# Dividing attention outputs by the softmax sums, which pass through DRAM, instead of scaling the probabilities

## The chip, the core and the metric

The kernel runs on one core of a Trainium2 chip. The metric is device time in microseconds (us), the median of the runs of one program. Five engines work side by side, each through its own instructions in a fixed order: TensorE (PE, with its weight loads as PEld), VectorE (DVE), ScalarE (ACT), GpSimd (POOL) and SyncE (SP, which here only issues DMAs). An engine that comes to an instruction whose inputs are not ready waits, and all that stands behind it waits too.

## The reference

One layer of a decoder on 16 meta tokens and 512 real ones, 1024 features wide, in float32: a gated feed-forward block, a token mixer with two attention branches, a second feed-forward block. The change is in the two attentions.

```python
def one_block(args):                                   # forgetting attention ("fox"), 8 heads of 64
    s = jnp.einsum('bqhd,bkhd->bhqk', qi, k) * scale
    s = s + cqi[..., :, None] - c_k[:, :, None, :]
    s = jnp.where(mask[None, None], s, NEG)
    pr = jax.nn.softmax(s, axis=-1)
    return jnp.einsum('bhqk,bkhd->bqhd', pr.astype(v.dtype), v)
...
# sliding window ("swa"), 8 query heads on 2 key heads, with a sink per head
mx = jnp.maximum(jnp.max(s, axis=-1, keepdims=True), sink)
pr = jnp.exp(s - mx)
pr = pr / (jnp.sum(pr, axis=-1, keepdims=True) + jnp.exp(sink - mx))
out = (jnp.einsum('bngrqk,bnkgd->bnqgrd', pr[..., :2 * BLOCK], vb)
       + jnp.einsum('bngrqm,bmgd->bnqgrd', pr[..., 2 * BLOCK:], vm))
...
y = jax.nn.sigmoid(ga) * (o_fox @ w_branch_fox) + jax.nn.sigmoid(gb) * (o_swa @ w_branch_swa)
return y @ w_out
```

## The kernel before

[...] A factor is split in a high half (a cast, `hi`, by ACT, L133) and a low half (what the cast left, `lo`, by DVE, L140), and PE adds high by high, high by low and low by high (`prod`, L301, L302, L304). Weights come from DRAM by SP in pieces of up to 512 KB into `raw`, which has three buffers (L252, L206); ACT makes `wh` from it, DVE `wl`, and a buffer comes free, and the next load goes out, when `wl` is made.

The program runs through the first feed-forward block, the projections and attentions of the mixer, the gates and output products, and the second feed-forward block. The attentions are sixteen units of work, first eight of `fox_pair` (two heads and two blocks of 128 queries; `p` counts the pairs of heads, `ip` the pairs of blocks, 1 before 0), then eight of `swa_unit` (four heads `g` and one block `i`). Each unit has these steps:

- `scores`: PE multiplies queries and keys (L1292 in fox, L301 to L304 in swa); DVE adds bias and mask, scales, writes the score tile `t` and its negated row maximum `nmx` (L1310, L1460); then `normalise`, which the change takes apart. There ACT makes the exponentials in place and their row sums `l` (L1209, a sum per query, and the queries lie on the partitions), DVE inverts the sums (L1210) and scales each tile by its own (L1212).
- `turn`: PE transposes `t` by a product with the identity (L1337 and L1350 in fox, L1473 in swa), ACT and DVE split the result in `pH` and `pL`. Now the keys lie on the partitions.
- `values`: PE multiplies `pH` and `pL` with the values `v` (L1359, L1364, L1365; L1488, L1490). The two halves of the partitions of the result are added into the output `oA` by ACT (L1105, a copy to `hsq`) and DVE (L1106). In `oA` the features lie on the partitions and the queries along the row, so a query's sum is no longer a scalar of a partition.

Between these steps stand fills, pieces of projections and gate products that have nothing to do with the unit (`weave`, L57): the turn and the values of a unit come after the scores of the next one, with fills between. The projections end in `head_norm`: ACT squares (L1057), DVE sums and adds (L1058, L1059), POOL takes the power (L351), DVE scales into `qn` (L1073). Within this frame the instructions of all engines are laid out when the program is built, by when each is thought to be ready, so that a changed step can move its neighbours. Loads and stores of ACT and SP stand in the same fixed order as the rest of their engine's work.

A tile `zA` takes the gates later; its rows 6 and 7 hold biases for fox, and its rows 0 to 3 are unused until the gates are made. After the attentions ACT reads `xg` from DRAM (L1700) into room that the attention's tiles leave.

Of the kernel before, what the change touches and what calls it, by code (L numbers as in the profile page):

```python
# [11 lines left out]
F32 = mybir.dt.float32  # L12
# [7 lines left out]
P = 128  # L20
# [5 lines left out]
NB = S // P  # L26
# [56 lines left out]
def kernel(  # L83
# [32 lines left out]
    def nm(s):  # L116
        nid[0] += 1
        return f"{s}_{nid[0]}"
# [339 lines left out]
    class Units:  # L458
# [5 lines left out]
        def new(self, tag, bufs, w=1):  # L464
            return self.pool.tile([P, w * self.th], F32, tag=tag, name=nm(tag), bufs=bufs)
# [633 lines left out]
    def both_halves(o, rows_, ps):  # L1099

        other = slice(64 - rows_.start, 128 - rows_.start)
        tmp = new("hsq", [P, 256], F32, 3)[rows_, :256]
        if len(ps.shape) > 2:
            tmp = tmp.rearrange("p (a q) -> p a q", q=P)
        A.copy(tmp, ps[other])  # L1105
        V.tensor_tensor(out=o, in0=ps[rows_], in1=tmp, op=ALU.add)  # L1106
# [95 lines left out]
        G.tensor_copy(lt[:, S:], ct[:, :M])  # L1202
        A.dma_start(cbd[0::2], lt[0:8:2])

    def normalise(parts):

        l = new("l", [P, 4], F32, 2)[:, : len(parts)]
        for j, (t, nmx) in enumerate(parts):
            shared["exp"] = A.activation(t, t, AF.Exp, bias=nmx, scale=-1.0, accum_out=l[:, j : j + 1])  # L1209
        V.reciprocal(l, l)  # L1210
        for j, (t, _) in enumerate(parts):
            V.tensor_scalar(t, t, l[:, j : j + 1], None, op0=ALU.mult)  # L1212


    cbs = {}
# [33 lines left out]
    def fox_pair(box, p, ip, before):  # L1249
# [7 lines left out]
        def scores():  # L1257
            before()
            q, k = box["q"], box["k"]
            main, last = cbs[p]  # L1260
            a, b = [main[:, :MAIN], last[:, : 2 * P]], [main[:, MAIN : 2 * MAIN], last[:, 2 * P :]]
            if ip:
                blocks = [
                    [[(P + M, MAIN, 0, 0, a[0])], [(0, MAIN, 0, 0, b[0])]],
                    [
                        [(LAST, LAST, 0, 2 * P, a[0][:, P:]), (M, 2 * P, 0, 0, a[1])],
                        [(0, LAST, 0, 0, b[0]), (LAST, 2 * P, 0, LAST, b[1])],
                    ],
                ]
            else:  # L1270
                w = 2 * P - P - M
                blocks = [
                    [[(3 * P + M - w, 2 * P, w, 0, a[1])], [(0, 2 * P, 0, 0, b[1])]],
                    [[(LAST, LAST, 0, 0, a[0][:, P:])], [(0, LAST, 0, 0, b[0])]],
                ]
            if ip:
                room = [new("t", [P, 1092], F32) for _ in range(2)]
            else:
                t = new("t0", [P, 2 * (keys[0] + keys[1] + M)], F32, 1)
                room = [t[:, : 2 * keys[0] + M], t[:, 2 * keys[0] + M :]]  # L1280
            for t, nk in zip(room, keys):
                G.memset(t[:, nk : nk + M], 0.0)
                ts_.append(t)
            pss = {}
            for b, block in enumerate(blocks):
                i = 2 * ip + b
                for pi in range(len(block[0])):
                    two = pss[b, pi] = psum(), psum()
                    for qx, kx in ((0, 0), (0, 1), (1, 0)):
                        for hb, ps, spans in zip(half, two, block):  # L1290
                            c0, w = spans[pi][:2]
                            PE.matmul(  # L1292
                                ps[:, :w],
                                q[qx][hb, hp, P * i : P * i + P],
                                k[kx][hb, hp, c0 : c0 + w],
                                start=qx + kx == 0,
                                stop=qx == 1,
                            )
            parts = []
            for hh in range(2):  # L1300
                for b, block in enumerate(blocks):
                    nk = keys[b]
                    t = ts_[b][:, (nk + M) * hh : (nk + M) * hh + nk]
                    nmx = new("nmx", [P, 2], F32, 8)
                    init = 3.0e38
                    for pi, (_, w, skip, to, cb) in enumerate(block[hh]):
                        n = min(w - skip, nk)
                        if not ip and b == 0:
                            n = nk
                        V.tensor_tensor_reduce(  # L1310
                            out=t[:, to : to + n],
                            in0=pss[b, pi][hh][:, skip : skip + n],
                            in1=cb[:, :n],
                            scale=-0.125,
                            scalar=init,
                            op0=ALU.add,
                            op1=ALU.min,
                            accum_out=nmx[:, pi : pi + 1],
                        )
                        init = nmx[:, pi : pi + 1]  # L1320
                    parts.append((t, init))
            for hh in range(2):
                normalise(parts[2 * hh : 2 * hh + 2])

        def column(hh, j, b):

# [28 lines left out]
        def values(hh):  # L1355
            v = box["v"]
            pv = psum()
            h0 = P * (2 * hp + hh)
            PE.matmul(pv[:, : 2 * P], v[:, 0, h0 : h0 + P], pts[0][:, : 2 * P], start=True, stop=False)  # L1359
            for j in range(1, nt):  # L1360
                pH, pL, c0 = pts[j]
                st = v[:, j, h0 : h0 + P]
                a = P if j == nt - 1 else 0
                PE.matmul(pv[:, a:256], st, pH[:, c0 + a : c0 + 256], start=False, stop=False)  # L1364
                PE.matmul(pv[:, a:256], st, pL[:, c0 + a : c0 + 256], start=False, stop=j == nt - 1)  # L1365
            both_halves(oA[half[hh], 0, p, 2 * P * ip : 2 * P * (ip + 1)], half[hh], pv[:, :256])

        return [scores] + [lambda f=f, hh=hh: f(hh) for hh in range(2) for f in (turn, values)]

# [61 lines left out]
    def swa_unit(box, qbox, g, i, before):  # L1431
# [8 lines left out]
        def scores():  # L1440
# [3 lines left out]
            for hp in range(2):  # L1444
                t2 = room[:, 546 * hp : 546 * hp + 546]
                for hh in (2 * hp, 2 * hp + 1):
# [16 lines left out]
                        )  # L1463
                        init = nmx[:, pi : pi + 1]
                    ts_.append((t, init))
            normalise(ts_)
            ts_[:] = [t for t, _ in ts_]

        def turn():
            for tt, c0 in tiles:  # L1470
# [12 lines left out]
        def values():  # L1483
            v = box["v"]
            pv = psum()
            for j, ((tt, c0), (pH, pL)) in enumerate(zip(tiles, pts)):
                st = v[:, tt, P * g : P * g + P]
                PE.matmul(pv, st, pH, start=j == 0, stop=False)  # L1488
                if tt:
                    PE.matmul(pv, st, pL, start=False, stop=j == len(tiles) - 1)  # L1490
            pvv = pv.rearrange("p (a b q) -> p a b q", b=2, q=P)
            for par in range(2):
                hb = slice(64 * par, 64 * par + 64)
                both_halves(o[hb, :, P * i : P * i + P], hb, pvv[:, :, par])

        return [scores, turn, values]

# [520 lines left out]
```

## Time and profile before

| what | us |
|---|---|
| median of three runs | 1078.03 (1077.87 to 1078.66) |
| the profiled execution | 1079.11 |
| its span, first to last instruction | 1076.5 |
| first scores of fox (L1292) | from 412.5 |
| first scores of swa (L1460) | from 520.1 |
| last of swa's scores begins (L1460) | 586.2 |
| load of xg (L1700) | 597.0 |

The granted clock of PE is 1.00 all through. In a row of a timeline the first number is the start and the second the duration, both in us; then come engine, line, operation, what is written and read, the shape, and in brackets the idle time of the engine just before and what ended it. In a row of groups the numbers behind the bar are the busy time in us and the mean of one in ns. "q" behind an engine marks what its sequencer issues. Line numbers are those of the kernel before, except where the changed program is shown.

### The profile page before, as it was taken

What the parts mean: (1) busy time and instruction counts of PE and PEld (TensorE: products, weight loads), DVE (VectorE), ACT (ScalarE), POOL (GpSimd) and SP (SyncE); (2) the same over time, 40 slices, a digit from 0 to 9 for tenths busy, and PEclk for the clock granted to TensorE, in tenths of its full rate; (3) what the DMA queues carried; (4) which work ended last, traced back from release to release, by engine and by line L of the source; (5) the groups of instructions that cost most, each with busy time, mean ns of one, the idle gap of its engine ahead of it and who ended that gap; (6) DMA issues with size and microseconds to landing.
All of it is one profiled execution on the core that took longest, in us unless ns stands there. A gap on an engine that the chain in (4) does not pass through costs nothing.

```text
span 1076.5 us, 22257 instructions
## 1 busy us (share of the span) xinstructions
PE 1063.5 (99%) x8515; PEld 1030.4 (96%) x8515; DVE 891.7 (83%) x1725; ACT 654.0 (61%) x1235; POOL 211.1 (20%) x280
## 2 busy tenths in 40 slices
PE   8999999999999999999999999999999999999998
PEld 8999999999999999999877799999999999999998
DVE  7988878888889678789897799688989788887895
ACT  7667456656666455556657776455665466645664
POOL 3011111121124442332200110001122211221120
PEclk9999999999999999999999999999999999999999
DMA  8787777688776314212211874557688877877763
GB/s 283 198 219 161 188 191 197 152 218 218 176 180 176 121 60 129 73 58 80 81 59 50 237 185 118 195 186 199 172 201 179 192 191 182 176 187 195 159 125 102
DMA packets 112299, 173.57 MB, mean 161 GB/s; under 512 B 10865, under 2 KB 59249, under 8 KB 111809
## 3 DMA queue, kind: packets, MB, share of 16 engines
q1 hardware_dynamic: 74032, 122.03, 35.7%
q0 software_dynamic: 28768, 37.83, 22.7%
q10 hardware_dynamic: 9392, 12.29, 3.6%
q8 instruction: 66, 1.08, 0.4%
q14 instruction: 41, 0.33, 0.1%
HBM read 167.89 MB, written 6.32 MB: 162 GB/s over the span
## 4 chain that ended last, share of the span: by engine, by line
PE 45%; DVE 5%; ACT 3%; DMA 2%; issue 1%; POOL 0%; ACTq 0%; DVEq 0%; POOLq 0%
PE ps L301 8%; PE ps L304 8%; PE ps L302 8%; PE pt L301 6%; PE pt L302 6%; PE pt L304 6%; DMA raw<-in_wout_dram 1%; DVE wl L140 1%; ACT wh L133 1%; DMA xg<-h1d 1%; ACT t L1209 1%; DVE pL L140 1%; PE ps L1473 0%; ACT xg L1728 0%; PE ps L1933 0%
## 5 line engine op out<-in xcount | busy, mean ns | idle before, releaser
L301 PE MATMUL ps<-x,wh 128*128 128x256 f32 (+2 forms) x768 | 219.7, 286 | 0.1
L302 PE MATMUL ps<-x,wh 128*128 128x256 f32 (+2 forms) x768 | 218.9, 285 | 0.5 <-DVE x L142 0.4
L304 PE MATMUL ps<-x,wl 128*128 128x256 f32 (+2 forms) x768 | 218.9, 285 | 0.0
L140 DVE TENSOR_TENSOR wl<-raw,wh 128x1024 fp32r<-128x1024 f32 (+3 forms) x125 | 149.9, 1200 | 43.9 <-ACT wh L133 42.6
L133 ACT CAST wh<-raw 128x1024 fp32r<-128x1024 f32 (+3 forms) x125 | 128.4, 1029 | 89.0 <-PE ps L302 52.3
L301 PEld LDWEIGHTS ps<-x,wh 128*128 128x128 f32 x768 | 144.7, 189 | 1.7 <-ACT hT L686 0.3
L302 PEld LDWEIGHTS ps<-x,wh 128*128 128x128 f32 x768 | 144.5, 188 | 1.4 <-DVE x L142 0.9
L304 PEld LDWEIGHTS ps<-x,wl 128*128 128x128 f32 x768 | 144.6, 188 | 0.8
L301 PE MATMUL pt<-x,wh 128*128 128x256 f32 (+2 forms) x424 | 125.3, 297 | 0.5 <-ACT wh L133 0.5
L304 PE MATMUL pt<-x,wl 128*128 128x256 f32 (+2 forms) x424 | 124.6, 294 | 0.0
L302 PE MATMUL pt<-x,wh 128*128 128x256 f32 (+2 forms) x392 | 112.6, 287 | 0.0
L133 ACT CAST wh<-tc 128x1024 fp32r<-128x1024 f32 (+1 forms) x70 | 71.8, 1026 | 65.5 <-DVE tc L234 54.4
L140 DVE TENSOR_TENSOR wl<-tc,wh 128x1024 fp32r<-128x1024 f32 (+1 forms) x70 | 83.4, 1192 | 32.4 <-ACT wh L133 32.1
L301 PE MATMUL ps<-acts,wh 128*128 128x264 f32 (+1 forms) x352 | 100.5, 286 | 0.3
L304 PE MATMUL ps<-acts,wl 128*128 128x264 f32 (+1 forms) x352 | 99.9, 284 | 0.0
L302 PE MATMUL ps<-acts,wh 128*128 128x264 f32 (+1 forms) x352 | 99.6, 283 | 0.0
L140 DVE TENSOR_TENSOR wl<-rawC,wh 128x1024 fp32r<-128x1024 f32 (+1 forms) x70 | 84.1, 1201 | 5.8 <-ACT wh L133 5.4
L133 ACT CAST wh<-rawC 128x1024 fp32r<-128x1024 f32 (+1 forms) x70 | 71.6, 1022 | 22.6 <-PE pt L302 17.6
L301 PEld LDWEIGHTS pt<-x,wh 128*128 128x128 f32 x424 | 80.0, 189 | 2.9 <-ACT wh L133 0.7
L304 PEld LDWEIGHTS pt<-x,wl 128*128 128x128 f32 x424 | 79.8, 188 | 2.1
L302 PEld LDWEIGHTS pt<-x,wh 128*128 128x128 f32 x392 | 73.8, 188 | 0.6
L301 PEld LDWEIGHTS ps<-acts,wh 128*128 128x128 f32 x352 | 66.5, 189 | 1.0 <-DVE h2T L918 0.7
(441 smaller groups left out, 3236.1 us busy)
## 6 DMA issues: line engine op xcount, KB each, us to landing
rawC<-in_w1i_dram SPq DMA_DIRECT2D x20, 512.0 KB, 4.3
raw<-in_w1i_dram SPq DMA_DIRECT2D x40, 256.0 KB, 4.2
raw<-in_w2i_dram SPq DMA_DIRECT2D x40, 256.0 KB, 3.5
rawC<-in_w2i_dram SPq DMA_DIRECT2D x20, 512.0 KB, 4.2
raw<-in_wm_dram SPq DMA_DIRECT2D x18, 512.0 KB, 4.5
raw<-in_wout_dram SPq DMA_DIRECT2D x16, 512.0 KB, 4.3
rawD<-in_w1i_dram SPq DMA_DIRECT2D x20, 256.0 KB, 4.3
raw<-in_w1i_dram POOLq DMA_DIRECT2D x20, 256.0 KB, 5.1
```

Source lines behind the costliest of these rows:

```text
L133: return A.copy(o, i)
L140: return V.tensor_tensor(out=o, in0=i, in1=h, op=ALU.subtract)
L301: PE.matmul(ps, sH, mH, start=first, stop=False, **more)
L302: PE.matmul(ps, sH, mL, start=False, stop=False, **more)
L304: shared["mm"] = PE.matmul(ps, sL, mH, start=False, stop=last, **more)
L1209: shared["exp"] = A.activation(t, t, AF.Exp, bias=nmx, scale=-1.0, accum_out=l[:, j : j + 1])
```

## The change

The probabilities are no longer scaled. ACT's exponentials go as they are through the transposes and the products with `v`, and the output `oA` is multiplied by the inverse sums, one product of 128 partitions by 256 a unit. For this the inverse sums of a unit (four a partition, 128 queries on the partitions) have to stand along the row and be the same on the 64 partitions of a head. SP writes them to a small tensor `rld` in DRAM, ordered by head and query, 512 runs of 4 bytes, and reads them back twice, once for each half of the partitions, with a step of 0 over the partitions, into `r`. For fox `r` lies in rows 0 to 3 of `zA`, for swa in a tile that fox's second units leave (`t0`), in three places in turn. The product is put off by one unit: `settle` runs at the end of a unit's values the product that the unit before owes. The last unit has nothing behind it, and scales its probabilities as before (`divide_now`).

```diff
-    def normalise(parts):
-
-        l = new("l", [P, 4], F32, 2)[:, : len(parts)]
+    owed = []
+
+    def exponentials(parts):
+
+        l = new("l", [P, 4], F32, 2)
         for j, (t, nmx) in enumerate(parts):
             shared["exp"] = A.activation(t, t, AF.Exp, bias=nmx, scale=-1.0, accum_out=l[:, j : j + 1])
         V.reciprocal(l, l)
+        return l
+
+    def divide_now(parts):
+
+        l = exponentials(parts)
         for j, (t, _) in enumerate(parts):
             V.tensor_scalar(t, t, l[:, j : j + 1], None, op0=ALU.mult)
+
+    def divide_later(parts, o, r, heads, runs):
+
+        l = exponentials(parts)
+        d = dp.tile([4, P], F32, name=nm("rld"))
+        flat = lambda *dims: bass.AP(tensor=d.tensor, offset=d.offset, ap=[list(x) for x in dims])
+        SP.dma_start(flat((1, P), (P, 4)), l)
+        cols, step = runs
+        for par in range(2):
+            src = bass.AP(tensor=d.tensor, offset=d.offset + heads * par, ap=[[0, 64], [step, 2 * P // cols], [1, cols]])
+            SP.dma_start(r[64 * par : 64 * par + 64], src)
+
+        def does():
+            V.tensor_tensor(out=o, in0=o, in1=r, op=ALU.mult)
+
+        return does
+
+    def settle(then=None):
+
+        for f in owed:
+            f()
+        owed[:] = [then] if then else []
...
-            for hh in range(2):
-                normalise(parts[2 * hh : 2 * hh + 2])
+            qs = slice(2 * P * ip, 2 * P * ip + 2 * P)
+            r = zA[:, p, qs].rearrange("p (a c) -> p a c", a=1)
+            o = oA[:, 0, p, qs].rearrange("p (a c) -> p a c", a=1)
+            ts_.append(divide_later(parts, o, r, 2 * P, (2 * P, 2 * P)))
...
             both_halves(oA[half[hh], 0, p, 2 * P * ip : 2 * P * (ip + 1)], half[hh], pv[:, :256])
+            if hh:
+                settle(ts_[-1])
...
-            normalise(ts_)
-            ts_[:] = [t for t, _ in ts_]
+            if (g, i) == (1, NB - 1):
+                divide_now(ts_)
+                ts_[:] = [t for t, _ in ts_] + [None]
+                return
+            if "r" not in shared:
+                shared["r"] = new("t0", [P, 864], F32, 1)
+            u = 2 * P * ((NB * g + i) % 3)
+            r = shared["r"][:, u : u + 2 * P].rearrange("p (a c) -> p a c", a=2)
+            does = divide_later(ts_, o[:, :, P * i : P * i + P], r, P, (P, 2 * P))
+            ts_[:] = [t for t, _ in ts_] + [does]
...
                 both_halves(o[hb, :, P * i : P * i + P], hb, pvv[:, :, par])
+            settle(ts_[-1])
```

The lines move: L1209 becomes L1211, L1210 becomes L1212, L1310 L1339, L1359 L1390, L1364 L1395, L1365 L1396; the write is L1226, the reads L1230, the product L1233.

How this moves instructions is shown at three places. The first is DVE in the fifth unit of fox (third pair of heads, `ip` 1, at 475 us of the profile), from its last scores to a low half `pL` that the values of the unit before need, before the change:

```order
L1210 RECIPROCAL l_6472<-l_6472 128x2
L1058 TENSOR_REDUCE hss_6498<-hsq_6497 128x2
L1212 TENSOR_SCALAR t_6434<-t_6434,l_6472 128x400
L1212 TENSOR_SCALAR t_6435<-t_6435,l_6472 128x528
L1210 RECIPROCAL l_6478<-l_6478 128x2
L1059 TENSOR_SCALAR hss_6498<-hss_6498,r1sq 128x2
L1212 TENSOR_SCALAR t_6434<-t_6434,l_6478 128x400
L1212 TENSOR_SCALAR t_6435<-t_6435,l_6478 128x528
L1073 SCALAR_TENSOR_TENSOR qn_6378<-hsq_6375,r_4883,hss_6381 16x2x64 x2
L1106 TENSOR_TENSOR oA<-ps_6507,hsq_6513 64x256
L140 TENSOR_TENSOR pL_6531<-ps_6529,pH_6530 128x384
```

The same place in the changed program, where L1212 is the reciprocal:

```order
L1058 TENSOR_REDUCE hss_6490<-hsq_6489 128x2
L1059 TENSOR_SCALAR hss_6490<-hss_6490,r1sq 128x2
L1073 SCALAR_TENSOR_TENSOR qn_6372<-hsq_6369,r_4883,hss_6375 16x2x64 x2
L1212 RECIPROCAL l_6466<-l_6466 128x4
L1106 TENSOR_TENSOR oA<-ps_6499,hsq_6505 64x256
L140 TENSOR_TENSOR pL_6523<-ps_6521,pH_6522 128x384
```

The four scalings are gone, the one reciprocal left stands behind the pair of `qn`, and `pL` follows. The second place is PE at the values that need this `pL`, among the fills of a projection (`ps` from `wh`, `wl` and `x`), before the change:

```order
L1359 MATMUL pt_6560<-pH_6390,v_4889 128x256
L1364 MATMUL pt_6560<-pH_6530,v_4889 128x256
L301 MATMUL ps_6569<-wh_6043,x_4304 128x256
L302 MATMUL ps_6569<-wl_6044,x_4304 128x256
L304 MATMUL ps_6569<-wh_6043,x_4308 128x256
L301 MATMUL ps_6569<-wh_6043,x_4304 128x256
L302 MATMUL ps_6569<-wl_6044,x_4304 128x256
L1365 MATMUL pt_6560<-pL_6531,v_4889 128x256
L1364 MATMUL pt_6560<-pH_6530,v_4889 128x128
L1365 MATMUL pt_6560<-pL_6531,v_4889 128x128
L304 MATMUL ps_6569<-wh_6043,x_4308 128x256
```

And in the changed program:

```order
L1390 MATMUL pt_6552<-pH_6384,v_4889 128x256
L1395 MATMUL pt_6552<-pH_6522,v_4889 128x256
L1396 MATMUL pt_6552<-pL_6523,v_4889 128x256
L1395 MATMUL pt_6552<-pH_6522,v_4889 128x128
L1396 MATMUL pt_6552<-pL_6523,v_4889 128x128
L301 MATMUL ps_6562<-wh_6037,x_4304 128x256
L302 MATMUL ps_6562<-wl_6038,x_4304 128x256
L304 MATMUL ps_6562<-wh_6037,x_4308 128x256
L301 MATMUL ps_6562<-wh_6037,x_4304 128x256
L302 MATMUL ps_6562<-wl_6038,x_4304 128x256
L304 MATMUL ps_6562<-wh_6037,x_4308 128x256
```

The five fills that stood ahead of the first product with `pL` now stand behind the unit's products. The third place is SP's queue in the middle of fox, which held weight loads alone; in the changed program it holds:

```order
L1226 DMA rld_5949<-l_5943 128x4x1
L1230 DMA zA<-rld_5949 64x256 x2
L252 DMA raw_6041<-in_wm_dram 128x1024
L252 DMA raw_6047<-in_wm_dram 128x1024
L1226 DMA rld_6196<-l_6190 128x4x1
L1230 DMA zA<-rld_6196 64x256 x2
L252 DMA raw_6344<-in_wm_dram 128x1024
L252 DMA raw_6350<-in_wm_dram 128x1024
L1226 DMA rld_6472<-l_6466 128x4x1
L1230 DMA zA<-rld_6472 64x256 x2
L252 DMA raw_6742<-in_wg_dram 128x1024
```

A write that waits for DVE and two reads that wait for the write now stand ahead of the loads of `raw`, which keep their own order.

## The prediction

> **What bounds the kernel now.** I read the page first (which engine is full, which chain ended last), then the nine 20 us stretches in which the attention units lie, then what TensorE (PE) waits for there, and only then single instructions. In the first two rows each engine's busy time is followed by its share of the span.
>
> ```profile
> PE 1063.5 (99%) x8515; PEld 1030.4 (96%) x8515; DVE 891.7 (83%) x1725; ACT 654.0 (61%) x1235; POOL 211.1 (20%) x280
> PE 45%; DVE 5%; ACT 3%; DMA 2%; issue 1%; POOL 0%; ACTq 0%; DVEq 0%; POOLq 0%
> ```
>
> PE is busy 99% of the span, and of the chain that ended last PE has 45% against 5% for VectorE (DVE). So an edit that only takes work off DVE pays exactly where PE waits for DVE, and nowhere else. The next two rows are the last 20 us of the attention and the sum of the nine stretches from 415 to 595 us (length, PE, PEld, DVE, ACT, POOL busy; granted clock; DMA share).
>
> ```profile
> 575.00:595.00 20.00, 19.31 (x109) 14.89 (x108) 15.56 (x42) 15.65 (x36) 0.71 (x1) 1.00 0.16 53
> sum 180.00, PE 176.95 PEld 156.73 DVE 150.30 ACT 114.71 POOL 32.48; mean PE 19.66 PEld 17.41 DVE 16.70 ACT 12.75 POOL 3.61
> ```
>
> PE stands idle for 180.00 - 176.95 = 3.05 us of the attention, although DVE is busy 83% of it. The idle time of the last 20 us, 0.69 us, lies in the last unit, which keeps its division. What PE waited for there (total, times, longest):
>
> ```profile
> PE pt L1365 <- DVE pL L140: 1.0, 3, 0.5
> PE ps L1292 <- DVE qn L1073: 0.5, 1, 0.5
> PE pt L1488 <- ACT pH L133: 0.5, 1, 0.5
> PE ps L1473 <- DVE t L1212: 0.3, 1, 0.3
> PE pt L1350 <- DVE qn L1073: 0.3, 1, 0.3
> PE pt L1490 <- DVE pL L140: 0.2, 1, 0.2
> ```
>
> L1488 and L1490 are the last unit's. Of the rest, 2.1 us in six waits, 1.3 us depends on how full DVE is (L1365 waits for the low halves pL, L1473 for the scaled tile itself). The two waits for qn do not: ahead of the 0.5 us one DVE itself had been idle, waiting for ScalarE (ACT).
>
> ```profile
> 435.72 0.42 DVE L1058 TENSOR_REDUCE hss<-hsq 128x4 f32<-128x256 f32 x1 [0.37 <-ACT hsq L1057]
> ```
>
> **What is removed from DVE.** The groups of the attention, with busy us and mean ns:
>
> ```profile
> L1212 DVE TENSOR_SCALAR t<-t,l 128x273 f32<-128x273 f32 (+3 forms) x64 | 20.2, 368 | 0.5
> L1210 DVE RECIPROCAL l<-l 128x2 f32<-128x2 f32 (+1 forms) x24 | 4.0, 165 | 5.0 <-ACT t L1209 4.0
> L1106 DVE TENSOR_TENSOR oA<-ps,hsq 64x256 f32<-64x256 f32 x12 | 5.0, 418 | 1.4 <-ACT hsq L1105 1.2
> ```
>
> Of 64 scalings of the probabilities, 4 stay (last unit): 20.2 x 60/64 = 18.9 us go. Eight of the 24 reciprocals go, since a fox unit now inverts four sums at once: 8 x 0.165 = 1.3 us. Fifteen products of 128 partitions by 256 come. No such product stands in the trace, and the nearest is the sum of two 256-wide operands in L1106, 0.42 us: 15 x 0.42 = 6.3 us. (That one reads PSUM and the new one SBUF alone; the bounds 0.37, the mean scaling, and 0.47, as far above, move the sum by 0.8 us either way.) DVE is lighter by 18.9 + 1.3 - 6.3 = 13.9 us, 8% of the 180 us. That is not the gain: PE waits for DVE only where the rows above say so.
>
> **What that frees on PE.** Waits shown understate what is lost, since a matmul's end is modelled:
>
> ```profile
> 476.12 0.48 ACT L133 CAST pH<-ps 128x384 fp32r<-128x384 f32 x1
> 475.21 0.82 DVE L1212 TENSOR_SCALAR t<-t,l 128x400 f32<-128x400 f32 x2
> 476.15 0.83 DVE L1212 TENSOR_SCALAR t<-t,l 128x400 f32<-128x400 f32 x2
> 476.38 0.75 POOL L351 TENSOR_TENSOR hss<-hss,nhalf 128x2 f32<-128x2 f32 x1 [1.01 <-DVE hss L1059]
> 477.76 0.54 DVE L140 TENSOR_TENSOR pL<-ps,pH 128x384 fp32r<-128x384 f32 x1
> 477.62 0.28 PE L301 MATMUL ps<-wh,x 128*128 128x256 f32 x1
> 477.74 0.28 PE L302 MATMUL ps<-wl,x 128*128 128x256 f32 x1
> 478.35 0.39 PE L1365 MATMUL pt<-pL,v 128*128 128x256 f32 x1 [0.33 <-DVE pL L140]
> ```
>
> Matmuls of 256 columns start 0.12 us apart; here 0.61 us pass, so 0.49 is lost where 0.33 is shown: 0.16 hides in each wait. The two other waits for pL (1.0 - 0.33 = 0.67) and the one for the scaled tile (0.3) are then worth 0.97 + 3 x 0.16 = 1.45 us. I let all of it go: at each, the scalings stand right ahead of the late instruction on DVE and take longer than the wait. For the scaled tile, whose row follows, the transposes can start when the exponentials end instead of after a reciprocal and the first scalings:
>
> ```profile
> 535.73 1.18 DVE L1212 TENSOR_SCALAR t<-t,l 128x273 f32<-128x273 f32 x4
> 536.24 1.05 PE L1473 MATMUL ps<-ident,t 128*128 128x128 f32 x4 [0.27 <-DVE t L1212]
> ```
>
> **What the new order takes back.** PE's instructions are the same in number, but the order is made anew at about eight places, since the program's order follows from when its parts are thought to be ready. At 477 us (shown in the section on the change) the five matmuls of the projection that stood between L1364 and L1365 now stand behind L1365. Their cover, 5 x 0.12 = 0.58 us, is gone. Against that pL comes earlier, but not by the 1.65 us of scalings: the qn pair ahead of it waits for GpSimd's power of hss, 0.75 us in the rows above, so I put pL 0.3 us earlier. Net: 0.58 - 0.3 = 0.28 us lost there. At 480 us the same five-matmul cover goes from ahead of the three L1350 transposes, whose bank is freed by qn and not by a scaling; as everything there runs 0.3 us earlier and PE 0.28 us later, I add 0.05. At 502 us four of the fills that stood before L1359 and four before L1365 now follow:
>
> ```profile
> 502.29 0.54 DVE L140 TENSOR_TENSOR pL<-ps,pH 128x384 fp32r<-128x384 f32 x1
> 503.03 0.28 PE L1365 MATMUL ps<-pL,v 128*128 128x256 f32 x1
> ```
>
> PE would come to L1365 eight times 0.12 us earlier, at 502.1, with pL there at 502.83 in the old timing. With the scalings out, pL is bound by ACT's pH and comes at about 502.4: 0.3 us lost. Together 0.63 us, between nothing (if pL keeps ahead) and 2 x 0.58 + 8 x 0.12 = 2.1 us (if nothing comes earlier).
>
> **The tail.** The product of the last but one unit now stands on DVE between the last unit's pL and the gates, where DVE works without a gap up to the last sums, and behind those ACT issues the load of xg:
>
> ```profile
> 595.55 0.41 DVE L1106 TENSOR_TENSOR oA<-pt,hsq 64x256 f32<-64x256 f32 x1
> 596.98 0.83 ACTq L1700 DMA_DIRECT2D xg<-h1d  x2
> ```
>
> Between nothing and one product (0.42); I take 0.2 us.
>
> **The round trip through DRAM.** Forty-five DMAs are added to SP's queue, three a unit: a write of 512 single values that waits for the reciprocal, and two broadcasts that wait for it to land. The nearest DMAs (KB each, us from issue to landing) are one of 1024 runs of 64 bytes (bm), one of 512 such runs (cb, 32 KB), and, as the far ends, the largest write to DRAM and the slowest read of its kind:
>
> ```profile
> bm<-biasd POOLq DMA_DIRECT2D x1, 64.0 KB, 3.1
> cb<-biasd ACTq DMA_DIRECT2D x2, 32.0 KB, 2.9
> biasd<-vecd SPq DMA_DIRECT2D x8, 256.0 KB, 6.4
> zA<-cbd ACTq DMA_DIRECT2D x4, 256.0 KB, 5.2
> ```
>
> I take 3.1 + 2.9 and about 1 us for three issues, 7 us; the upper end is 6.4 + 5.2 + 1 = 12.6 us. The product of a unit stands one unit later in the order. The shortest distance is that of the first unit of the second group, whose reciprocal and place of the product are:
>
> ```profile
> 563.26 0.18 DVE L1210 RECIPROCAL l<-l 128x4 f32<-128x4 f32 x1 [0.89 <-ACT t L1209]
> 572.88 0.43 DVE L1106 TENSOR_TENSOR oA<-pt,hsq 64x256 f32<-64x256 f32 x1 [0.56 <-ACT hsq L1105]
> ```
>
> 573.31 - 563.44 = 9.9 us, so 7 us are covered. Behind SP's waits stand the weight loads. The one with the least room is sent at 445.04 (first of this row), when its buffer, one of three, comes free, and its cast starts at 463.82:
>
> ```profile
> 445.04 3.07 SPq L252 DMA_DIRECT2D raw<-in_wm_dram  x2
> 463.82 1.04 ACT L133 CAST wh<-raw 128x1024 fp32r<-128x1024 f32 x1
> raw<-in_wm_dram SPq DMA_DIRECT2D x8, 512.0 KB, 5.8
> ```
>
> That is 18.8 us, and such a load lands 5.8 us after its issue (median, last row). A delay of 2 to 4 us behind a write costs nothing.
>
> [...]
>
> **Sum.** - 1.45 + 0.63 + 0.2 = -0.6 us. Against the profiled execution (1079.11 us: span 1076.5 and 2.6 around it) that is 1078.5; that execution is 1.1 us above the median of the three runs, 1078.03, so for a median I forecast **1077.4 us**. A measurement of this kernel can tell about 0.2%, 2.2 us, from no change (1075.9 to 1080.2).
>
> **Rivals.**
>
> *DVE's relief cures every wait and the new order costs nothing.* Then all of the 3.05 - 0.69 = 2.4 us that PE shows idle goes, with six hidden parts of 0.16: 3.3 us, 1074.7. For it: DVE is the releaser in five of the six rows. Against it: the qn waits follow ACT and GpSimd, and cover was taken away. Less complete, 2.3 us and up, it is still faster by the bound. 16%.
>
> *The round trip is longer than the distance.* DVE works in order, so a product that waits holds up the pL behind it, and PE behind that. It decides from 9.9 us on. At 12.6 us the tightest unit stands 2.7 us; of the sliding-window units, which follow each other every 7 to 9 us, some three more would stand 1 to 2 us, 7 us in all. DVE has 180.00 - 150.30 = 30 us of idle time and 14 more from the change, which takes up perhaps a third: +4.7 - 0.6, 1082. For it: no 4-byte write is in the trace. Against it: the 64-byte rows. 11%.
>
> *The new order costs its upper end.* -1.45 + 2.1 + 0.4 = +1.1 us, 1079.1, no change by the bound. 9%.
>
> That the change doesn't do what it says can be excluded: the built program has the 60 scalings no more.
>
> **Numbers.** The forecast has 64%; with the third rival the time stays within 0.2% in 73%; faster 16%; slower 11%. For 8 in 10 the range reaches from 1075.0, into the first rival, to 1079.8, beyond the third; the second is left out.
>
> **What would show it.** Right: L1233 products of about 0.4 us with no wait for a DMA; L1473 without its wait for t; DVE's sum in the attention near 136 us; PE's idle time there about as before, with L1365 at 477 and 502 among what waits. Wrong: idle time of DVE that a DMA of zA or t ends (second rival), PE's idle time under 1 us (first), or a cast of wh that waits for its load, which nothing above allows for.

## The result, and the profile after

The changed kernel takes 1107.13 us (median of six runs, 1101.97 to 1108.73) against 1078.01 us (six runs) before: a ratio of 1.0261, 95% interval 1.0246 to 1.0275. It is slower by 29 us, where 1077.4 us were forecast. The profiled execution of it took 1108.25 us, its span is 1106.3. First the page of the changed kernel: busy time of the engines, and the chain that ended last by line.

```profile
PE 1074.7 (97%) x8515; PEld 1038.5 (94%) x8515; DVE 880.8 (80%) x1672; ACT 654.8 (59%) x1235; POOL 210.1 (19%) x280
PE ps L301 13%; PE ps L302 13%; PE ps L304 13%; PE pt L301 11%; PE pt L304 11%; PE pt L302 11%; DMA rld<-l 5%; DVE wl L140 2%; DMA raw<-in_wout_dram 1%; DMA zA<-rld 1%; ACT wh L133 1%; DMA rawC<-in_wg_dram 1%; PE ps L345 1%; ACT t L1211 1%; DMA t<-rld 1%
```

DVE lost 10.9 us of work (891.7 before), as meant. But the write of the sums (rld<-l) now has 5% of the chain, some 55 us, and before, the chain, which could be followed back to 472 us, held one DMA of the attention, a weight load with 3 us. Next, stretches of 20 us of the changed kernel (length, PE, PEld, DVE, ACT, POOL busy; granted clock; DMA share; GB/s).

```profile
435.00:455.00 20.00, 14.46 (x99) 13.47 (x99) 11.14 (x35) 6.85 (x15) 5.32 (x9) 0.83 0.16 38
575.00:595.00 20.00, 16.87 (x92) 13.45 (x91) 9.02 (x36) 10.45 (x29) 0.00 (x0) 0.91 0.21 34
595.00:615.00 20.00, 14.80 (x75) 10.74 (x75) 9.31 (x25) 6.82 (x17) 0.00 (x0) 0.91 0.22 66
```

One of them as it was before the change:

```profile
435.00:455.00 20.00, 19.45 (x158) 17.94 (x157) 17.20 (x53) 11.04 (x26) 5.15 (x9) 1.00 0.17 54
```

The loss is not spread. One stretch of fox has it (435 to 455: PE does 99 matmuls there, 158 before), then nothing until 555, then the sliding-window units that are left. The starts of the same instructions in the two traces, counted in order, say the same:

| instruction | before at | later after the change by |
|---|---|---|
| scores of fox (L1292), first | 412.55 | 0.1 |
| ... the 49th | 451.28 | 8.9 |
| ... the 109th | 506.20 | 9.1 |
| transposes of swa (L1473), the 25th | 546.44 | 8.3 |
| ... the 37th | 554.67 | 15.0 |
| ... the 61st | 572.64 | 19.7 |
| ... the 73rd | 581.87 | 24.6 |
| ... the 85th | 589.67 | 29.2 |

What DVE and PE waited for in the attention of the changed kernel (total, times, longest), and what SP's queue waited for:

```profile
DVE oA L1233 <- DMA t<-rld: 26.4, 6, 6.8
DVE oA L1233 <- DMA zA<-rld: 7.7, 1, 7.7
PE ps L1321 <- DVE pL L140: 5.4, 1, 5.4
PE pt L301 <- DVE pL L140: 4.5, 1, 4.5
SPq L1230 <- DMA rld<-l: 104.2, 11, 11.6
```

The products (L1233) wait 34.1 us for reads of the sums, one of them in fox, the others in swa, and PE waits for the low halves behind them on DVE. SP stands 9.5 us, on average, at a read until the write before it has landed. SP's queue over three units:

```profile
559.98 0.38 SPq L1226 DMA_DIRECT2D rld<-l  x1
568.86 1.25 SPq L1230 DMA_DIRECT2D t<-rld  x2
570.20 0.54 SPq L252 DMA_DIRECT2D raw<-in_wg_dram  x1
570.79 0.42 SPq L1226 DMA_DIRECT2D rld<-l  x1
580.82 1.24 SPq L1230 DMA_DIRECT2D t<-rld  x2
582.15 0.54 SPq L252 DMA_DIRECT2D raw<-in_wbr_dram  x1
582.75 0.43 SPq L1226 DMA_DIRECT2D rld<-l  x1
594.38 2.19 SPq L1230 DMA_DIRECT2D t<-rld  x2
596.66 0.55 SPq L252 DMA_DIRECT2D raw<-in_wbr_dram  x1
597.26 0.42 SPq L1226 DMA_DIRECT2D rld<-l  x1
```

A write is sent, 9 to 12 us later its reads, then a weight load, then the next write: SP carries one unit's round trip at a time, 10.8 to 14.5 us from write to write. DVE's product behind the reads of 594.38 starts 16 us after the write:

```profile
598.74 0.43 DVE L1233 TENSOR_TENSOR oA<-oA,t 128x256 f32<-128x256 f32 x1 [6.75 <-DMA t<-rld]
```

### The profile page after: what moved, and what is told of

Same layout as the page of the kernel before. It is cut to its first block, busy times and chain, and to the rows that moved or that the text cites. A ratio compares the mean times of both kernels' runs of the same rounds, so it can differ in the third digit from the quotient of the medians.

```text
span 1106.3 us, 22314 instructions
## 1 busy us (share of the span) xinstructions
PE 1074.7 (97%) x8515; PEld 1038.5 (94%) x8515; DVE 880.8 (80%) x1672; ACT 654.8 (59%) x1235; POOL 210.1 (19%) x280
## 3 DMA queue, kind: packets, MB, share of 16 engines
q0 software_dynamic: 28768, 37.83, 21.8%
## 4 chain that ended last, share of the span: by engine, by line
PE 76%; DMA 9%; DVE 7%; ACT 3%; issue 2%; SPq 1%; POOL 0%; ACTq 0%; DVEq 0%; POOLq 0%
PE ps L301 13%; PE ps L302 13%; PE ps L304 13%; PE pt L301 11%; PE pt L304 11%; PE pt L302 11%; DMA rld<-l 5%; DVE wl L140 2%; DMA raw<-in_wout_dram 1%; DMA zA<-rld 1%; ACT wh L133 1%; DMA rawC<-in_wg_dram 1%; PE ps L345 1%; ACT t L1211 1%; DMA t<-rld 1%
```

## The experiments

Three readings were open: the products wait in DVE's order for a slow landing; SP's queue is the limit, whoever reads the sums; or the new order of instructions costs the time.

### Without readers, and without DMAs

The first run lets the products multiply the output by itself:

```diff
-            V.tensor_tensor(out=o, in0=o, in1=r, op=ALU.mult)
+            V.tensor_tensor(out=o, in0=o, in1=o, op=ALU.mult)
```

The second does the same, and the three DMAs are gone:

```diff
-        SP.dma_start(flat((1, P), (P, 4)), l)
...
-            SP.dma_start(r[64 * par : 64 * par + 64], src)
```

> The changed program with every write, read, wait of SP and instruction in its place, but the product multiplies the output by itself and so doesn't read r (the outputs are not divided). Landing theory (DVE stands in its order until the reads of a unit have landed, PE behind it): the seven waits of L1233, 34.1 us, go, the granted clock is 1.00 in every stretch, and the time is 1075 to 1080 us. Queue theory (SP stands at each write until it has landed, and sends the weight loads behind it late): weight loads go out as late as in the changed kernel, casts wait for them, and 1085 to 1100 us remain. Order theory (the new order of instructions costs the time): nothing of the order changes, so the time stays above 1095 us.

> The changed program without the 45 DMAs, with products that multiply the output by itself (the outputs are not divided); the order on PE, ACT and POOL is the same. This is the prediction's sum without the round trip: - 1.45 + 0.63 + 0.2 = -0.6 us, 1077.4 us. Landing theory: within 1 us of the run with the unread DMAs. Queue theory: faster than that run by what the late loads cost, 5 us or more. Order theory: above 1095 us as well.

Unread: 1102.84 us, ratio 1.0229 (1.0215 to 1.0243). No DMAs: 1075.36 us, 0.9979 (0.9970 to 0.9988). The second result disposes of the order theory, since it has the new order and no loss; the first alone, above the range of the queue theory, would have spoken for it. The first shows that the loss does not need the products: with no product waiting, nearly all of it stayed. Waits of ACT, DVE and SP's queue in the run with unread DMAs:

```profile
ACT t L1211 <- DMA rld<-l: 22.2, 4, 7.1
DVE spare L1737 <- DMA t<-rld: 5.5, 1, 5.5
SPq L1230 <- DMA rld<-l: 137.9, 14, 12.2
```

The wait had moved. The sums `l` have two buffers, so the exponentials of a unit wait until the write of two units before has left its buffer, and that write goes out 9 to 13 us after its reciprocal in the last units, because SP stands at the writes ahead of it.

### Which property of the write is slow

In place of the one write come five forms, in turn over the units: 128 runs of 16 bytes, 4 of 512 bytes, 512 of 4 bytes with a gap (32 floats: 128 bytes), 128 of 4 bytes, and 512 of 4 bytes to on-chip memory, 16 bytes apart, and from there to DRAM:

```diff
-        SP.dma_start(flat((1, P), (P, 4)), l)
...
+        if form == 0:
+            SP.dma_start(flat((4, P), (1, 4)), l)
+        elif form == 1:
+            SP.dma_start(flat((P, 4), (1, P)), ident[:4])
...
+            SP.dma_start(flat((gap, P), (gap * P, 4)), l)
...
+            SP.dma_start(flat((1, P)), l[:, 0])
...
+            SP.dma_start(onchip[:, 0:16:4], l)
+            SP.dma_start(flat((4, P), (1, 4)), onchip[:, 0:16:4])
```

The run on spacing has the form with a gap alone, with gaps of 1, 2, 4, 8 and 16 floats in turn.

> The products read no DMA (the outputs are not divided), and the write takes five forms in turn, three units each; its landing is read from when SP issues the read that waits for it. The form of the change, 512 runs of 4 bytes to neighbouring places, lands in 8 to 12 us. Forms: 128 runs of 16 bytes; 4 runs of 512 bytes; 512 runs of 4 bytes that lie 128 bytes apart or more; 128 runs of 4 bytes; 512 runs of 4 bytes to on-chip memory, and from there to DRAM. If the number of runs sets the landing: 2 to 3.5 us for 128 runs of either size and 2 to 3 for 4 runs, 8 to 12 for the spaced form and on chip. If it is that several runs fall into one stretch of DRAM and must follow each other: 8 to 12 for both forms of 128 runs, 2 to 3 for 512-byte runs, for the spaced form and on chip. If every write to DRAM takes so long to be reported: 8 to 12 for all but the on-chip one.

> Products without reads (the outputs are not divided), and 512 runs of 4 bytes whose places lie 4, 8, 16, 32 and 64 bytes apart, in turn, three units each. If the cost is per run in a shared stretch, the landing falls with the spacing: 8 to 12 us, 5 to 7, 3.5 to 4.5, 2.7 to 3.2, 2.3 to 2.5. If only runs that lie in one 64-byte line disturb each other however few they are: 8 to 12 up to 32 bytes apart and 2 to 3 at 64. If it is the number of runs: 8 to 12 throughout, which the 128-byte spacing (1.9 to 3.4 us) speaks against.

SP's queue in the run with forms shows how this is read: 128 runs of 16 bytes, 512 of 4 bytes that lie 128 bytes apart, 128 of 4 bytes side by side, each with the reads that wait for it.

```profile
419.37 0.33 SPq L1231 DMA_DIRECT2D rld<-l  x1
422.45 1.39 SPq L1251 DMA_DIRECT2D zA<-rld  x2
442.18 0.38 SPq L1236 DMA_DIRECT2D rld<-l  x1
444.05 1.12 SPq L1251 DMA_DIRECT2D zA<-rld  x2
459.00 0.33 SPq L1239 DMA_DIRECT2D rld<-l  x1
466.97 1.09 SPq L1251 DMA_DIRECT2D zA<-rld  x2
```

From a write's issue to that of its reads, in us, three units each (the reads' wait may include more than the landing, so these are upper bounds):

| write | three units |
|---|---|
| 512 runs of 4 bytes, side by side | 8.7, 11.3, 9.7 |
| 512 runs of 4 bytes, 8 bytes apart | 7.8, 4.9, 7.4 |
| 16 bytes apart | 3.0, 4.5, 3.9 |
| 32 bytes apart | 3.4, 2.4, 3.6 |
| 64 bytes apart | 1.8, 1.9, 3.4 |
| 128 bytes apart | 1.9, 3.4, 2.9 |
| 128 runs of 4 bytes, side by side | 8.0, 7.6, 8.5 |
| 128 runs of 16 bytes, side by side | 3.1, 4.5, 3.2 |
| 512 runs of 4 bytes to on-chip memory, 16 bytes apart | 2.1, 4.7, 4.6 |
| from there to DRAM, 512 pieces of 4 bytes, side by side | 8.7, 8.7, 7.1 |

It is not the number of runs: 128 neighbours take 8 us, 512 runs 64 bytes apart take 2.4. Whether it is DRAM alone these runs don't tell: on chip the places lay 16 bytes apart, and at that distance DRAM took no longer. What exceeds about 2 us roughly halves with each doubling of the distance (means 9.9, 6.7, 3.8, 3.1, 2.4 us). That is the fall with the spacing that was expected if the cost is per run in a shared stretch; the runs show the times and not this mechanism, nor how long such a stretch would be. The form of 4 runs of 512 bytes gave no reading: its source waited for nothing, and the writes went out at the kernel's start (from 16.1 us on). The times of the two programs, 1077.59 and 1074.32 us, are of one run each; they show no loss like that of the change, in programs that read nothing of r and write side by side in some of the units only.

### The change with other runs

One line gives runs of 16 bytes (each query then gets a sum that belongs to another):

```diff
-        SP.dma_start(flat((1, P), (P, 4)), l)
+        SP.dma_start(flat((4, P), (1, 4)), l)
```

Runs of 8 bytes, with each query its own sum, need the columns of l in another order, and a product that steps by two:

```diff
-        l = exponentials(parts)
+        l = exponentials(parts, (lambda j: j) if runs[0] == 2 * P else (lambda j: 2 * (j % 2) + j // 2))
...
-        SP.dma_start(flat((1, P), (P, 4)), l)
+        SP.dma_start(flat((2, P), (2 * P, 2), (1, 2)), l.rearrange("p (h a) -> p h a", a=2))
...
-            src = bass.AP(tensor=d.tensor, offset=d.offset + heads * par, ap=[[0, 64], [step, 2 * P // cols], [1, cols]])
+            src = bass.AP(tensor=d.tensor, offset=d.offset + 2 * P * par, ap=[[0, 64], [1, 2 * P]])
...
-            V.tensor_tensor(out=o, in0=o, in1=r, op=ALU.mult)
+            V.tensor_tensor(out=o, in0=o, in1=r.rearrange("p (q a) -> p a q", a=2), op=ALU.mult)
```

> The changed program with one line changed: the write keeps the order of l, so it is 128 runs of 16 bytes in place of 512 of 4 (each query then gets a sum that belongs to another). Everything else, waits and reads and products, stays. If the slow write of neighbouring 4-byte runs is the one cause: it lands in 3 to 4.5 us, SP's part of a unit is about 6 us, no product waits, the granted clock is 1.00, and the time is that of the run without DMAs, 1075 to 1078 us. If the reads or SP's waits as such cost: 1085 us or more.

> The change with right numbers and 256 runs of 8 bytes: the two sums that a half of the partitions needs lie side by side, the read stays two blocks of 1 KB, and the product steps through r by two. If each run that falls into the same stretch of DRAM adds to the landing: 5 to 7 us for the write, SP's part of a unit 7 to 9 us, 1075 to 1079 us, with at most one or two products that wait. If any run under 16 bytes is as slow as one of 4: 1095 to 1107 us.

16 bytes: 1076.18 us, 0.9979 (0.9969 to 0.9989). 8 bytes: 1077.34 us, 0.9989 (0.9979 to 0.9999). SP's wait for the write with 16 bytes:

```profile
SPq L1230 <- DMA rld<-l: 30.4, 15, 3.6
```

The same with 8 bytes, and then one product of that run:

```profile
SPq L1230 <- DMA rld<-l: 57.0, 15, 6.2
```

```profile
573.06 0.43 DVE L1233 TENSOR_TENSOR oA<-oA,t 128x256 f32<-128x256 f32 x1
```

SP stands 2.0 and 3.8 us a unit in place of 9.5, and no product has a wait in brackets. All the rest is the change as it was, with every engine's order the same, so the runs of 4 bytes are the cause of the whole loss. Of the versions that divide each query by its own sum, the one with 8 bytes is the fastest: 30 us under the change and, with an interval that ends just below 1, level with the kernel before or a trifle under it.

### How the slow write reaches the end of the kernel

Both runs leave the products unread and give l sixteen buffers; the first has no reads either, the second has them as in the change.

```diff
-        l = new("l", [P, 4], F32, 2)
+        l = new("l", [P, 4], F32, 16)
```

> The changed program with its fifteen writes of 512 runs of 4 bytes, no reads, products that read no DMA (the outputs are not divided), and sixteen buffers for l in place of two, so that nobody waits for a write. If the loss comes only through waits for the write: 1075 to 1077 us, as without any DMA. If the write under way holds up other transfers so that they come too late: weight loads that land in up to 10 us in place of 3 to 5, and 1080 us or more.

> The run with the unread DMAs (1102.8 us), with sixteen buffers for l in place of two, so that the exponentials no longer wait for a write two units back; SP's queue is as in the change. If SP's rate of one round trip per 11.5 to 12 us reached the engines there by the buffer of l alone (22.2 us of waits): 1076 to 1084 us, with what SP sends late at the end of the attention as the rest. If the weight loads that stand behind the writes cost the time: 1090 to 1103 us.

Writes alone: 1086.67 us, 1.0071 (1.0053 to 1.0089), though nobody waits for them. The place is the stretch of fox in which the changed kernel lost 9 us: the 49th scores of fox come 7.2 us late, the last transposes of swa 6.4, so the writes of swa cost nothing here. GpSimd's mask there needs a bias that ACT's queue loads into zA: here are the load and the mask before the change.

```profile
427.18 0.38 ACTq L1228 DMA_DIRECT2D zA<-cbd  x1
432.43 0.41 POOL L1232 TENSOR_SCALAR_AFFINE_SELECT zA<-zA 128x256 f32<-128x256 f32 x1 [2.80 <-DMA zA<-cbd]
```

The same two in the run with writes alone, and DVE's qn behind GpSimd:

```profile
424.89 0.38 ACTq L1258 DMA_DIRECT2D zA<-cbd  x1
436.29 0.41 POOL L1262 TENSOR_SCALAR_AFFINE_SELECT zA<-zA 128x256 f32<-128x256 f32 x1 [2.94 <-DMA zA<-cbd]
437.70 0.47 DVE L1073 SCALAR_TENSOR_TENSOR qn<-hsq,r,hss 16x256 f32<-16x256 f32 x1 [4.40 <-POOL hss L351]
```

And what PE waits for there:

```profile
PE ps L1322 <- DVE pL L140: 3.8, 1, 3.8
```

The same load takes 11.4 us in place of 5.3 while a write of 4-byte runs, sent at 423.17, is under way on the other queue; GpSimd's power, DVE's qn and PE follow. In the changed kernel the transfer that is held there is the first unit's read (sent at 426.05, product at 438.84, the next unit's write sent at 427.27).

The other run, 1102.26 us, 1.0207 (1.0176 to 1.0237), missed its 1076 to 1084. It lies in the range of late weight loads, but the trace shows another wait. The last stretch of the attention and the one behind it:

```profile
575.00:595.00 20.00, 19.49 (x109) 14.99 (x109) 14.76 (x39) 16.00 (x37) 0.00 (x0) 1.00 0.26 67
595.00:615.00 20.00, 7.09 (x31) 5.45 (x29) 1.45 (x4) 2.02 (x4) 0.00 (x0) 0.73 0.18 40
```

SP's last write and reads there, and the DVE instruction that waits for them:

```profile
601.27 0.43 SPq L1226 DMA_DIRECT2D rld<-l  x1
611.33 1.24 SPq L1230 DMA_DIRECT2D t<-rld  x2
616.16 2.50 DVE L1737 TENSOR_TENSOR spare<-x 128x512 f32<-128x512 f32 x4 [19.28 <-DMA t<-rld]
```

The attention runs at full speed (its last transposes come 0.1 us earlier than before the change), while SP falls behind by 2 to 6 us with each unit of swa: the last write leaves 21.8 us after its reciprocal. The next tile in the place of r has to wait for the last read, and 19.28 us are lost there at once. So the rate of the round trips sets the end, whatever waits for them: the products in the change, the buffers of l in the first run, the next tile here.

### More distance, and another queue

The reads of swa on GpSimd's queue (first and last run):

```diff
-            SP.dma_start(r[64 * par : 64 * par + 64], src)
+            (G if cols == P else SP).dma_start(r[64 * par : 64 * par + 64], src)
```

Products two units later (second and third run):

```diff
-        for f in owed:
-            f()
-        owed[:] = [then] if then else []
+        owed.append(then)
+        if len(owed) > 2 and owed[0]: owed[0]()
+        del owed[:-2]
```

Products bound behind the last sum (L1106) of the next unit (fourth and fifth; `shared["half"]` is that sum):

```diff
-        for f in owed:
-            f()
+        with after(shared["half"]):
+            [f() for f in owed]
```

In the second and third run the last two units divide at once, and the last three runs give l sixteen buffers.

> The reads of the sliding-window units go through GpSimd's queue, so that SP no longer stands at a write; the products read r as in the change. In the changed kernel a write left up to 7 us after its reciprocal, since SP stood at the write before. If that queueing makes most of the loss, the round trip is 10 + 4.8 = 14.8 us from the reciprocal, the seven sliding-window waits fall to about 1 us each, and the time is 1080 to 1088 us. If the landing alone makes it, the time stays at 1098 to 1107 us. Order theory: no change, 1107.

> The changed program with each product two units after its reciprocal in place of one (the last two units divide at once). Distance theory (the round trip is longer than the distance; my second rival): the distance goes from 10 to about 18 us and more, the waits of L1233 go, 1077 to 1082 us. Rate theory (SP can carry one unit's round trip per 11.5 to 12 us, the write's 10 us and 1.9 us of issues, while a sliding-window unit took 8.5 us before): the wait only moves, to the exponentials that need a buffer of l or to the product, and 1095 to 1105 us remain.

> Each product two units after its reciprocal, as before, but with four places for r in place of three (in the earlier run the reads of the third unit on went to the place of a product that had not been made, so it waited for those too and had the wrong sums) and sixteen buffers for l; the last two units divide at once. Distance theory: 1075 to 1080 us. Rate theory: a write leaves later than its reciprocal by about 3.5 us more with each sliding-window unit, so products wait from the third of these units on, 1085 to 1095 us.

> The changed program with each product bound behind the last sum of the next unit's values on DVE, so that it truly stands one unit after its own unit's values (in the program of the change, and in both runs with two units, the order that is made at build time puts it right behind its own unit's values, some 10 us after its reciprocal), and sixteen buffers for l. All results are divided rightly. Distance theory: the distance is now about 18 us against a round trip of 15, so the waits go and 1076 to 1081 us come. Rate theory: SP's chain of fifteen round trips at 11.5 to 12 us ends where it ended in the run with unread DMAs and sixteen buffers (last read landed at 616 us, 22 us after the last reciprocal but one should have had it), so 1095 to 1103 us remain, with the waits at the last products.

> The same with the reads of the sliding-window units on GpSimd's queue, so that SP can send each write when its reciprocal is made. Rate theory: SP's queue is the limit, and with it gone 1077 to 1086 us come, the rest being reads that a later write holds up (up to 11 us from issue to landing in the earlier run with GpSimd's queue). If the writes themselves cannot follow each other faster than one per 10 to 12 us whatever queue stands at them: 1090 to 1103 us.

| run | us | ratio, 95% |
|---|---|---|
| reads on GpSimd's queue | 1114.21 | 1.0357 (1.0326 to 1.0389) |
| two units, three places | 1124.99 | 1.0439 (1.0415 to 1.0463) |
| two units, four places | 1113.22 | 1.0316 (1.0297 to 1.0334) |
| bound behind the next unit | 1104.00 | 1.0225 (1.0192 to 1.0259) |
| the same, reads on GpSimd's queue | 1092.28 | 1.0133 (1.0116 to 1.0150) |

None of the first three lies in a range that was expected of it; the fourth lies 1 us above that of the rate theory. The two runs with two units test nothing of distance: where a product is written in the code doesn't hold it back, and the order made at build time put it right behind its own unit's values again. That it is so in the change as well came out here. Bound with an order constraint, it stands 19 us and more behind its reciprocal, and the time still is that of the run with unread DMAs: distance alone cures next to nothing (3 us), as the rate theory said. Its products wait for the backlog; DVE's waits for them, bound and on SP's queue:

```profile
DVE oA L1233 <- DMA t<-rld: 22.4, 5, 6.8
```

Bound, with the reads on GpSimd's queue, the same wait, and the two queues at two units:

```profile
DVE oA L1233 <- DMA t<-rld: 10.6, 5, 2.8
```

```profile
551.20 1.22 POOL L1230 DMA_DIRECT2D t<-rld  x2 [9.61 <-DMA rld<-l]
551.36 0.39 SPq L1226 DMA_DIRECT2D rld<-l  x1
563.81 1.17 POOL L1230 DMA_DIRECT2D t<-rld  x2 [11.40 <-DMA rld<-l]
559.35 1.04 SPq L1226 DMA_DIRECT2D rld<-l  x1
574.94 1.17 POOL L1230 DMA_DIRECT2D t<-rld  x2 [9.95 <-DMA rld<-l]
```

How long the reads take in that run, those of fox on SP's queue among them:

```profile
DMA to landing us min/median/max: 3.2/8.2/11.6
```

Taking SP's wait in swa away as well halves the loss (from 26 to 14 us), but no more, against the 1077 to 1086 expected: the reads, sent just ahead of the next write (551.20 and 551.36), now are held by it, with a median of 8.2 us to landing (4.0 in the bound run with all reads on SP's queue). That fits the 1114 us of GpSimd's queue alone, where reads took up to 10.5 us and the products had their short distance. Two things more stand in this trace. Six of the 14 us are lost before the first transposes of swa, in fox, whose reads stay on SP's queue. And the time lies in the range of the other reading, that the writes themselves can't follow each other faster, whatever queue waits for them. The trace speaks for that reading too: SP sends five writes 8 to 12 us apart, but their reads go out 12 to 16 us behind them. Of two writes whose landing it tells, the one with no other under way (542.21) took 8.7 us, the one behind another (579.73) 13.1. Three effects of one write, then: its landing, SP's rate behind it, and the transfers that it holds up, the next write among them. No run keeps the second apart from the last, and how the 29 us divide between them can't be said, since a wait taken from one falls to the next.

## Why the prediction was wrong

**What bounds the kernel, and what the relief is worth:** right, though too small. The work taken from DVE is as forecast, 13.9 us: in the run without DMAs these groups hold 6.3 + 2.8 + 1.2 = 10.3 us, where 20.2 + 4.0 stood before. (The sum over the nine stretches, in which overlapping instructions count once, fell from 150.3 to 140.1 us, not to the 136 that were named as a sign.)

```profile
L1233 DVE TENSOR_TENSOR oA<-oA 128x256 f32<-128x256 f32 x15 | 6.3, 419 | 0.3
L1212 DVE RECIPROCAL l<-l 128x4 f32<-128x4 f32 x16 | 2.8, 176 | 7.0 <-ACT t L1211 6.8
L1219 DVE TENSOR_SCALAR t<-t,l 128x273 f32<-128x273 f32 x4 | 1.2, 358 | 0.0
```

That run's 0.9979 is just at the 0.2% that the forecast took for no change. The forecast had -0.6 us; the trace of that run shows the attention 1.8 us shorter (its first scores come 0.26 us earlier than before, the last transposes 2.10). The term that was mis-sized is the sum of the named waits: the three places in fox came out at about nothing (0.1 us up to the last scores of fox), as the new order took back what the scalings gave, and 1.7 us came in swa, where only 0.3 + 0.16 had been counted. The tail's 0.2 us was nothing: the load of xg goes out 2.09 us earlier, as do the last transposes.

**The round trip through DRAM** is the step that failed: "I take 3.1 + 2.9 and about 1 us for three issues, 7 us; the upper end is 6.4 + 5.2 + 1 = 12.6 us". Against a distance of 9.9 us that made the round trip cost nothing in the sum. In the change it is 8 to 12 us for the write and 4.3 for a read (the median below), 14 to 16 us from the write to the products that wait in swa, beyond even the upper end.

```profile
t<-rld SPq DMA_DIRECT2D x14, 64.0 KB, 4.3
```

The rows that it was taken from were reads from DRAM in 64-byte runs, 3.1 us for the write too. The figure would have held for other writes: 4-byte runs that lie 64 bytes apart land in 2.4 us (a mean of three). Side by side they take four times as long. A bound made of "the largest write" was no bound, since size was not what mattered: the 2 KB of 4-byte neighbours took 8 to 12 us, the 256 KB written to biasd 6.4 before the change. Nor was it that the runs were small or many: the 128 runs of 16 bytes cost this kernel nothing (1076.18 us, 0.9979), and 512 runs of 4 bytes were not dear wherever they lay (2.4 us, 64 bytes apart).

**The distance** of 9.9 us was read off the order rightly, but "the product of a unit stands one unit later in the order" was not so: it stands behind its own unit's values.

**The second rival** is what happened, by its mechanism: products that wait for a DMA, pL behind them, PE behind that. The sign that was named for it, idle time of DVE that a DMA of zA or t ends, came with 34.1 us. Its price, 4.7 us, was too low sixfold. It took a wait of 1 to 3 us at four units; it left out that SP, which stands at each write, can't send the next one, so that a unit of 8.5 us cannot be shorter than a round trip of 12; that transfers take longer beside a write (11.4 us in place of 5.3 for the load of zA in the run with writes alone); and that PE's granted clock was 0.83 in the stretch in which it stood 5.4 us, 1.00 there before. "A delay of 2 to 4 us behind a write costs nothing" held for weight loads (no cast in the attention of the changed kernel waits for one), but the instruction queued behind SP's wait that mattered was the next write. Given 11%, it lay outside the range.

**The other rivals:** the relief that cures all (1074.7) is near the run without DMAs (1075.4), but by luck in part: PE's idle time in the nine stretches fell from 3.05 to 2.51 us and not to nothing, and of the 3.2 us by which that run's profiled span is shorter, 1.1 lie in a load of xg that took less long. The new order at its upper end is excluded by the same run.

## What to carry to other kernels

Before values are passed through DRAM, look at how many bytes lie side by side in each run of the write: with 8 bytes in place of 4, by choosing the order of the columns, this change goes from 29 us lost to nothing lost. For a wait on a queue, compare the time of one round with the time of one unit of the loop, and not only with the distance to the reader: here the queue, at about 12 us a round against 8.5 us a unit, was slower than the loop, the backlog was paid somewhere, and moving the reader (1104.00 us, 1107.13 in the change) only moved the place. And where an order is made at build time, a step written later in the code isn't later in the program unless a constraint says so.

## What was not expected of the hardware

A DMA write of 2 KB in 4-byte neighbours landed in 8 to 12 us, though the trace's packets of the one sent at 417.86 all fall between 418 and 420, six microseconds before the read that waits for it goes out. While one was under way, other transfers took longer, on SP's own queue (the longest 4096-byte packet, a piece of a weight load, between 415 and 590 us took 6.3 us in the changed kernel, 1.5 before) and on others (the load on ACT's queue above, 11.4 us in place of 5.3). And PE's waits were dearer than they look: where PE had stood 5.4 us, the granted clock of the stretch was 0.83, and the matmuls behind were longer (0.41 us, 0.28 before).

```profile
441.32 0.59 PE L1321 MATMUL ps<-kH,qH 64*128 64x272 f32 x1 [5.39 <-DVE pL L140]
443.81 0.41 PE L302 MATMUL pt<-wl,x 128*128 128x256 f32 x1
444.02 0.41 PE L304 MATMUL pt<-wh,x 128*128 128x256 f32 x1
```

The last two start 0.21 us apart, where 0.12 us was usual before.
